# A state space layer of a two-block model at batch 256 tokens: the scans over pairs of tokens

## The chip, the cores and the metric

The kernel runs on one core of a Trainium2 chip. Its time is the device time of one execution in microseconds; of several executions the median is given. A core has the engines TensorE (PE in the profile, its weight loads are PEld), VectorE (DVE), ScalarE (ACT), GpSimd (POOL) and SyncE (SP), which issues most of the transfers. Each works off a queue of its own in order, and they wait for each other by semaphores.

## The reference

The model has two FFN layers around an even and an odd mixer, and two further layers behind. The change is in the odd mixer's state space half (S5). It has 32 groups of 16 channels and 64 complex states; the kernel lays two of them on the 128 partitions and calls these 32 channels and 128 states one of its 16 groups. S is 256 tokens.

```python
u = zd.reshape(B, S, S5_GROUPS, S5_GROUP_CH).astype(jnp.float32)
lam = lax.complex(lam_re, lam_im)
dt = jnp.exp(log_dt)[:, None]
lam_bar = jnp.exp(lam * dt)
b_bar = ((lam_bar - 1.0) / lam)[..., None] * b_c
bu = jnp.einsum('gpc,bsgc->sbgp', b_bar, u.astype(jnp.complex64))
a = jnp.broadcast_to(lam_bar, (S, 1, S5_GROUPS, S5_STATE))
def combine(e1, e2):
    a1, b1 = e1
    a2, b2 = e2
    return a2 * a1, a2 * b1 + b2
_, states = lax.associative_scan(combine, (a, bu), axis=0)
y = jnp.einsum('gcp,sbgp->bsgc', c_c, states).real + d_skip * u
y = jax.nn.gelu(y.reshape(B, S, S5_WIDTH))
ab = y @ w_glu
y_d = ab[..., :S5_WIDTH] * jax.nn.sigmoid(ab[..., S5_WIDTH:])
return jnp.concatenate([y_c, y_d], axis=-1) @ w_out
```

So the state after token t is `lam_bar` times the state after t-1, plus `b_bar` times the token's input, and a token's output is the real part of C times its state, plus `d_skip` times its input. The other half of the mixer, `y_c`, is a pooling branch.

## The kernel before

All work is on one core and all 256 tokens are columns of one tile. Big products are split into a high and a low fp32r part of activation and weight (`xh`, `xl`, `wh`, `wl`, three matmuls a product; L251 is the helper that issues every such matmul). ScalarE makes `wh` (L160) and VectorE `wl` (L161) out of `raw`, which SyncE fetches (L143).

`s5_params` prepares the constants of the S5 half. It is a generator: `run` hands it to two FFN layers (`ffn1(0, 1)` and `ffn1(1, 0)`, until 690 us), which take a step of it at each `yield`, so that its work lies between theirs. For each of 16 groups i it makes a table `tab` with the sine and cosine of the state's angle at each of the 256 tokens (L729 to L737), further `rho` (the modulus of `lam_bar`), `fr`, `fi` (the factor of `b_bar`), `bexp` and out of it by transposes `bt` (the matrix of the drive, L775, L777), and `cw` (the matrix of the read, three copies: real, minus imaginary, minus real; fetched at L779, changed at L780 and L781).

`odd` is the mixer, from 690 to 809 us. Its input projections come first; `u` (tile `s5u`) is the S5 half's input, times the norm's factor `R` (L796). Then a loop of 19 steps runs over the 16 groups as a software pipeline. A group's steps are:

- `drive`: f32 matmuls out of 32 partitions of `u` (for two groups at a time, on two row groups of TensorE, into two PSUM banks).
- `turn`: VectorE multiplies the two halves of that PSUM bank with the table (L820, L821, 128x512), which turns the complex state back by its angle.
- `scan`: a sum and a difference (L825, L826), then two scans over 256 columns with the real factor `rho` (L829, L830). GpSimd multiplies one of the results with the table (`zi`, L832).
- `back`: VectorE does so with the other (`zr`, L838).
- `read`: four f32 matmuls with `cw` into 32 rows of `py`, a column group of TensorE (L844).
- `finish`, after each fourth group: `d_skip` (L849), gelu (L850), and the split into `yh`, `yl` (L267, L269).

Turnings of group n, the turning back of n-1, scans of n and the read of n-2 are issued in this order in step n. After each step one step of `pooling` is issued, the pooling branch: first its projection of the input (512 columns), then for each of four groups a product with the pooling matrix, `pl` (ScalarE, L869), a product with `pw`, `yc` (ScalarE, L873) and its halves `ch`, `cl` (L267, L269), and last `od_w_out` over `ch`, `cl`. After the loop come the gate's matmuls (`s5_w_glu` over `yh`, `yl`) and the second half of `od_w_out`. The scheduler of the framework sets the order on each engine out of what the code issues, so steps of one tile are moved among those of another.

## Time and profile before

| what | us |
| --- | --- |
| median of 3 runs (lowest, highest) | 3098.61 (3095.78, 3099.87) |
| profiled execution | 3096.39 |
| its span on the chip | 3094.6 |
| TensorE busy in the span | 3000.1 (97%) |
| VectorE busy | 2317.8 (75%) |
| ScalarE busy | 1874.5 (61%) |
| from `s5u` (L796) to the first matmul of the second `od_w_out` half | 706.26 to 797.78 |

Times in the profile count from the start of the span. An instruction's row gives its start, its length, engine, line, what it writes and reads (`out<-in`), the shape, and how many it stands for (x4: four in a row). In brackets stands for how long the engine had been idle before it, and who released it. Matmuls are pipelined, so the distance from start to start counts, not the length; an f32 matmul leaves two records, an fp32r one leaves one.

### The profile page before, as it was taken

Reading aid. Unit: us, or ns where it says so; the run is one execution under the profiler, and the core shown is the slowest. Engines: PE = TensorE matmul, PEld = TensorE weight load, DVE = VectorE, ACT = ScalarE, POOL = GpSimd, SP = SyncE. Lnnn points to the kernel's source line nnn. Section 1 sums busy time; section 2 is a strip of 40 time slices with the busy share of each in tenths; the row PEclk is TensorE's granted clock in tenths of the full one; section 3 lists DMA queues with packets and bytes.
Section 4 is the critical chain, followed back from the end, with each engine's and each line's share of the span. In section 5 each row is a group of like instructions: output and inputs, shape, how many; then the busy total and the mean of one; then the engine's idle time right before and its main releaser. Section 6 shows DMA issues by size and latency. Waiting matters only on the chain. (4 is left out here: it accounts for less than half of the span.)

```text
span 3094.6 us, 51454 instructions
## 1 busy us (share of the span) xinstructions
PE 3000.1 (97%) x20681; PEld 2715.5 (88%) x20681; DVE 2317.8 (75%) x3292; ACT 1874.5 (61%) x2593; POOL 174.9 (6%) x147
## 2 busy tenths in 40 slices
PE   8999999999999999999999999999999999999998
PEld 8997999995899889899998888988888887888886
DVE  6667787868775675566556665569999999999998
ACT  5556555552444665554546654458788778778776
POOL 1000000002102000012010000000000000000000
PEclk9999999999999999999999999999999999999999
DMA  6542455551455334454553334658998998999994
GB/s 254 205 163 99 180 187 181 200 212 57 164 191 194 123 126 147 167 192 163 191 191 123 124 134 180 235 218 316 363 371 335 364 358 343 363 363 342 358 370 157
DMA packets 97413, 696.49 MB, mean 225 GB/s; under 512 B 10880, under 2 KB 11232, under 8 KB 13456
## 3 DMA queue, kind: packets, MB, share of 16 engines
q1 hardware_dynamic: 95184, 685.81, 59.9%
q0 software_dynamic: 752, 3.98, 0.4%
q8 instruction: 164, 2.69, 0.3%
q10 hardware_dynamic: 1232, 3.34, 0.3%
q14 instruction: 81, 0.66, 0.1%
HBM read 692.05 MB, written 1.05 MB: 224 GB/s over the span
## 5 line engine op out<-in xcount | busy, mean ns | idle before, releaser
L161 DVE TENSOR_TENSOR wl<-raw,wh 128x1024 fp32r<-128x1024 f32 x1299 | 1580.4, 1236 | 491.4 <-ACT wh L160 456.5
L160 ACT ACTIVATE wh<-raw 128x1024 fp32r<-128x1024 f32 x1299 | 1361.9, 1060 | 762.0 <-PE pa L251 633.8
L251 PE MATMUL pa<-xh,wh 128*128 128x256 f32 x3072 | 862.4, 281 | 13.2 <-ACT wh L160 9.8
L251 PE MATMUL pa<-xl,wh 128*128 128x256 f32 x3072 | 860.6, 280 | 4.0 <-DVE xl L349 4.0
L251 PE MATMUL pa<-xh,wl 128*128 128x256 f32 x3072 | 858.7, 280 | 0.9 <-DVE wl L161 0.9
L251 PEld LDWEIGHTS pa<-xh,wh 128*128 128x128 f32 x3072 | 581.4, 189 | 18.1 <-ACT wh L160 9.8
L251 PEld LDWEIGHTS pa<-xl,wh 128*128 128x128 f32 x3072 | 581.5, 189 | 6.7 <-DVE xl L349 5.0
L251 PEld LDWEIGHTS pa<-xh,wl 128*128 128x128 f32 x3072 | 585.1, 190 | 1.9 <-DVE wl L161 1.5
L251 PE MATMUL pa<-wl,gxh 128*128 128x512 f32 x896 | 349.7, 390 | 1.6 <-DVE wl L161 1.5
L251 PE MATMUL pa<-wh,gxl 128*128 128x512 f32 x896 | 348.8, 389 | 0.0
L251 PE MATMUL pa<-wh,gxh 128*128 128x512 f32 x896 | 317.1, 389 | 0.0
L251 PE MATMUL pa<-hh,wl 128*128 128x256 f32 x880 | 245.2, 279 | 0.0
L251 PE MATMUL pa<-hl,wh 128*128 128x256 f32 x880 | 245.2, 279 | 0.0
L251 PE MATMUL pa<-hh,wh 128*128 128x256 f32 x880 | 245.0, 278 | 0.0
L251 PEld LDWEIGHTS pa<-wl,gxh 128*128 128x128 f32 x896 | 168.2, 188 | 40.1 <-DVE wl L161 5.2
L251 PEld LDWEIGHTS pa<-wh,gxh 128*128 128x128 f32 x896 | 168.1, 188 | 35.1
L251 PEld LDWEIGHTS pa<-wh,gxl 128*128 128x128 f32 x896 | 168.2, 188 | 34.6
L251 PE MATMUL pb<-wl,mhh 128*128 128x512 f32 x448 | 177.2, 396 | 1.1 <-DVE wl L161 1.1
L251 PE MATMUL pb<-wh,mhl 128*128 128x512 f32 x448 | 176.0, 393 | 0.0
L251 PEld LDWEIGHTS pa<-hh,wl 128*128 128x128 f32 x880 | 165.9, 189 | 0.1
L251 PEld LDWEIGHTS pa<-hl,wh 128*128 128x128 f32 x880 | 165.7, 188 | 0.0
L251 PEld LDWEIGHTS pa<-hh,wh 128*128 128x128 f32 x880 | 165.7, 188 | 0.0
(512 smaller groups left out, 3987.6 us busy)
## 6 DMA issues: line engine op xcount, KB each, us to landing
raw<-in_moe SPq DMA_DIRECT2D x336, 1024.0 KB, 6.2
raw<-in_dense SPq DMA_DIRECT2D x315, 1024.0 KB, 4.8
c_lay<-in_c_lay POOLq DMA_DIRECT2D x2, 1216.0 KB, 6.6
x<-in_xt SPq DMA_DIRECT2D x4, 256.0 KB, 5.6
raw<-in_dense SPq DMA_DIRECT2D x4, 256.0 KB, 6.7
w<-in_cw ACTq DMA_DIRECT2D x1, 1024.0 KB, 8.1
out_dram<-hx SPq DMA_DIRECT2D x2, 512.0 KB, 2.6
c_odd<-in_c_odd POOLq DMA_DIRECT2D x1, 768.0 KB, 4.5
```

What stands on the lines that cost most here:

```text
L160: self.nc.scalar.activation(h, src, AF.Copy)
L161: self.nc.vector.tensor_sub(l, src, h)
L251: self.nc.tensor.matmul(out, l, r, start=start, stop=stop, skip_group_check=True)
```

## The change

The state is now carried over two tokens at a time: 128 columns, one for each pair of tokens. With s(t) the state after token t, s(2m+1) = lam_bar^2 s(2m-1) + lam_bar b u(2m) + b u(2m+1). So

- `u` is stored by parity: [128, 4, 2, 128], first tokens and second tokens of all pairs (four VectorE products of 256 instead of two of 512).
- A second drive matrix with the factor `lam_bar` b (`gr`, `gi`) is made: `bexp1`, and `bt` holds both. A drive of two groups is eight matmuls of 128 columns (tokens 1 and 0 accumulated) instead of four of 256.
- `tab`, and all steps that make it, are 128 columns wide. The values of `lam_bar` come from a short calculation of their own (`one`) instead of 32 products of one column out of `tab`; `rho` is squared.
- `turn`, `scan`, `back` and `zi` take two groups at once: four turnings of 256 elements, a sum and a difference over both groups (2x128), four scans of 128 columns, one `zi` and one `zr` of 512. The loop has 10 steps, and takes two steps of `pooling` in each.
- `back` now joins `zr` and `zi` into one tile by a difference and a sum (L887, L888), so that a read is two matmuls a group and token. Second tokens are read by `cw`, first tokens by `cl` (C times `lam_bar`) from the state of the pair ahead of them (127 columns), and a direct product `d0` (C times b, a 128x128 matrix for each four groups) times the first tokens' input. `cl` costs six VectorE operations of 128x512, `d0` 32 matmuls of 32x32 at the boundary of FFN and mixer, and four copies by ScalarE; `cw` has no third copy any more.
- `cw` is fetched right after `s5b` and not after the transposes.
- `finish` writes `y` with a stride of two.
- `free=384` instead of 128 moves addresses alone.

```diff
+        tab = P2.tile([128, 16, 2, 128], F32, name="tab")
...
+        nc.scalar.activation(one[:, 1], one[:, 0], AF.Sin, scale=2 * math.pi * (1 - 2.0 ** -22))
+        io = io[:, 0:S:2]
...
+        cw = P2.tile([128, 2, 16, 32], F32, name="cw")
+        tc.keep_in_program_order(nc.scalar.dma_start(cw, self.a["s5c"]))
...
+        bt = P2.tile([128, 2, 2, 4, 128], F32, name="bt")
+        for tok, (mr, mi) in enumerate(((fr, fi), (gr, gi))):
...
+            bexps.append(bexp)
+            yield
+            for ri in range(2):
+                pt = self.pbank((128, 4, 128))
+                for j in range(4):
+                    nc.tensor.transpose(pt[:, j], bexp[:, ri, 4 * j:4 * j + 4].rearrange("p a b c -> p (a b c)"),
+                                        self.ident)
+                nc.scalar.activation(bt[:, tok, ri], pt, AF.Copy)
...
-        cw = P2.tile([128, 3, 16, 32], F32, name="cw")
-        tc.keep_in_program_order(nc.scalar.dma_start(cw[:, 0:2], self.a["s5c"]))
+
+
         V.tensor_scalar_mul(cw[:, 1], cw[:, 1], -1.0)
-        V.tensor_scalar_mul(cw[:, 2], cw[:, 0], -1.0)
-        self.s5 = dict(rho=rho_t, tab=tab, bt=bt, cw=cw)
+        cl = P2.tile([128, 2, 16, 32], F32, name="cl")
+        ct = P.tile([128, 16, 32], F32, name="s5ct")
+        bc = lambda v: v[:, :, None].to_broadcast([128, 16, 32])
+        for ri, op in enumerate((OP.add, OP.subtract)):
+            V.tensor_mul(cl[:, ri], cw[:, ri], bc(lr1))
+            V.tensor_mul(ct, cw[:, 1 - ri], bc(li))
+            V.tensor_tensor(cl[:, ri], cl[:, ri], ct, op=op)
+        yield
+        d0 = P2.tile([128, 4, 128], F32, name="d0")
+        tc.keep_in_program_order(nc.gpsimd.memset(d0, 0.0))
+        pt = self.pbank((128, 4, 32))
+        for i in range(16):
+            j, q = divmod(i, 4)
+            for ri in range(2):
+                nc.tensor.matmul(pt[32 * q:32 * q + 32, j], bexps[0][:, ri, i].rearrange("p b c -> p (b c)"),
+                                 cw[:, ri, i], start=j == 0 and ri == 0, stop=j == 3 and ri == 1,
+                                 skip_group_check=True, tile_position=(0, 32 * q))
+        for q in range(4):
+            r = slice(32 * q, 32 * q + 32)
+            nc.scalar.activation(d0[r, :, r], pt[r], AF.Copy)
+        self.s5 = dict(rho=rho_t, tab=tab, bt=bt, cw=cw, cl=cl, d0=d0)
...
-            u = P.tile([128, 4, S], F32, name="s5u")
+
+            u = P.tile([128, 4, 2, 128], F32, name="s5u")
+            apart = lambda t: t.rearrange("p (t r) -> p r t", r=2)
             bs = [self.proj_t([(w, idx, 512 + 256 * i, 256)], self.xh, self.xl) for i in range(2)]
             rc, R = factors()
             for i in range(2):
-                nc.vector.tensor_mul(u[:, 2 * i:2 * i + 2], bs[i], R[:, None, :].to_broadcast([128, 2, S]))
+                for n in range(2):
+                    nc.vector.tensor_mul(u[:, 2 * i + n], apart(bs[i][:, n]), apart(R))
...
-                bus = [self.pbank((128, 2, S)) for _ in range(2)]
+                bus = [self.pbank((128, 2, 128)) for _ in range(2)]
                 for ri in range(2):
-                    for n, bu in enumerate(bus):
-                        j, q = divmod(i + n, 4)
-                        r = slice(32 * q, 32 * q + 32)
-                        self.mm(bu[:, ri], s5["bt"][r, ri, j], u[r, j], True, True)
+                    for tok in range(2):
+                        for n, bu in enumerate(bus):
+                            j, q = divmod(i + n, 4)
+                            r = slice(32 * q, 32 * q + 32)
+                            self.mm(bu[:, ri], s5["bt"][r, tok, ri, j], u[r, j, 1 - tok], ri == 0 and tok == 0, tok == 1)
...
-            def turn(i, bu):
-
-                tb = s5["tab"][:, i]
+                return P.tile([128, 2, 2, 128], F32, name=n, tag="s5w", bufs=9)
+
+            def both(v):
+                return v[:, :, None, :].to_broadcast([128, 2, 2, 128])
+
+            def turn(i, bus):
+
                 a1, a2 = work("a1"), work("a2")
-                V.tensor_mul(a1, bu[:, 0, None, :].to_broadcast([128, 2, S]), tb)
-                V.tensor_mul(a2, bu[:, 1, None, :].to_broadcast([128, 2, S]), tb)
+                for n, bu in enumerate(bus):
+                    for ri, a in enumerate((a1, a2)):
+                        V.tensor_mul(a[:, n], bu[:, ri, None, :].to_broadcast([128, 2, 128]), s5["tab"][:, i + n])
                 return a1, a2
 
             def scan(i, a1, a2):
-                V.tensor_add(a1[:, 1], a1[:, 1], a2[:, 0])
-                V.tensor_sub(a1[:, 0], a2[:, 1], a1[:, 0])
+                V.tensor_add(a1[:, :, 1], a1[:, :, 1], a2[:, :, 0])
+                V.tensor_sub(a1[:, :, 0], a2[:, :, 1], a1[:, :, 0])
                 z = a2
-                rho = s5["rho"][:, i:i + 1].to_broadcast([128, S])
-                V.tensor_tensor_scan(z[:, 1], rho, a1[:, 0], 0.0, OP.mult, OP.add)
-                V.tensor_tensor_scan(z[:, 0], rho, a1[:, 1], 0.0, OP.mult, OP.add)
+                for n in range(2):
+                    rho = s5["rho"][:, i + n:i + n + 1].to_broadcast([128, 128])
+                    V.tensor_tensor_scan(z[:, n, 1], rho, a1[:, n, 0], 0.0, OP.mult, OP.add)
+                    V.tensor_tensor_scan(z[:, n, 0], rho, a1[:, n, 1], 0.0, OP.mult, OP.add)
                 zi = work("zi")
-                nc.gpsimd.tensor_mul(zi, z[:, 1, None, :].to_broadcast([128, 2, S]), s5["tab"][:, i])
+                nc.gpsimd.tensor_mul(zi, both(z[:, :, 1]), s5["tab"][:, i:i + 2])
                 return z, zi
 
             def back(i, z, zi):
 
                 zr = work("zr")
-                V.tensor_mul(zr, z[:, 0, None, :].to_broadcast([128, 2, S]), s5["tab"][:, i])
-                return zr, zi
-
-            def read(i, zr, zi, py):
-                o = py[32 * (i % 4):32 * (i % 4) + 32, :S]
-                for n, (c, z) in enumerate(((0, zr[:, 1]), (1, zr[:, 0]), (2, zi[:, 0]), (1, zi[:, 1]))):
-                    nc.tensor.matmul(o, cw[:, c, i], z, start=n == 0, stop=n == 3, skip_group_check=True,
-                                     tile_position=(0, 32 * (i % 4)))
+                V.tensor_mul(zr, both(z[:, :, 0]), s5["tab"][:, i:i + 2])
+                V.tensor_sub(zr[:, :, 1], zr[:, :, 1], zi[:, :, 0])
+                V.tensor_add(zr[:, :, 0], zr[:, :, 0], zi[:, :, 1])
+                return zr
+
+            def read(i, zr, py):
+
+                if i % 4 == 0:
+                    self.mm(py[:, 0], s5["d0"][:, i // 4], u[:, i // 4, 0], True, False)
+                for ri in range(2):
+                    for c, o, t in ((cw, py[:, 1], 128), (s5["cl"], py[:, 0, 1:128], 127)):
+                        for n in range(2):
+                            q = 32 * ((i + n) % 4)
+                            nc.tensor.matmul(o[q:q + 32], c[:, ri, i + n], zr[:, n, 1 - ri, 0:t], start=False,
+                                             stop=ri == 1, skip_group_check=True, tile_position=(0, q))
 
             def finish(j, py):
                 y = W.tile([128, S], F32, name="y", tag="t256", bufs=4)
-                V.scalar_tensor_tensor(y, u[:, j], self.vec("s5d", j), py[:, :S], op0=OP.mult, op1=OP.add)
+                V.scalar_tensor_tensor(apart(y), u[:, j], self.vec("s5d", j), py, op0=OP.mult, op1=OP.add)
...
+            z, x, py = {}, {}, None
+            for m in range(8 + 2):
+                i = 2 * m
+                if m < 8:
+                    a = turn(i, drive(i))
+                if 0 <= m - 1 < 8:
+                    x[m - 1] = back(i - 2, *z.pop(m - 1))
+                if m < 8:
+                    z[m] = scan(i, *a)
+                if 0 <= m - 2 < 8:
+                    i -= 4
                     if i % 4 == 0:
+                        py = self.pbank((128, 2, 128))
+                    read(i, x.pop(m - 2), py)
+                    if i % 4 == 2:
+                        finish(i // 4, py)
+                for _ in range(2):
+                    next(steps, None)
```

What moves in the order, at three places (`pb` and `pa` are PSUM banks). TensorE at the boundary from the FFN (`pa<-hh`) to the mixer's first projection (`pa<-xh`), before:

```order
L251 MATMUL pa_8213<-hh_6082,wl_8303 128x256
L775 MATMUL pb_8378<-c_all_101,bexp_8199 128x128 [waits Pool_49]
L775 MATMUL pb_8378<-c_all_101,bexp_8199 128x128 x3
L775 MATMUL pb_8384<-c_all_101,bexp_8199 128x128 x4
L251 MATMUL pa_8421<-xh_108,wh_8302 128x256 [waits PE_49]
```

and after:

```order
L251 MATMUL pa_8198<-hh_6087,wl_8288 128x256
L795 MATMUL pb_8362<-c_all_101,bexp0_8186 128x128 [waits Pool_49]
L795 MATMUL pb_8362<-c_all_101,bexp0_8186 128x128 x3
L795 MATMUL pb_8368<-c_all_101,bexp0_8186 128x128 x4
L795 MATMUL pb_8387<-c_all_101,bexp1_8374 128x128 [waits DVE_49,Pool_49]
L795 MATMUL pb_8387<-c_all_101,bexp1_8374 128x128 x3
L795 MATMUL pb_8393<-c_all_101,bexp1_8374 128x128 [waits DVE_49]
L795 MATMUL pb_8393<-c_all_101,bexp1_8374 128x128 x3
L816 MATMUL pb_8410<-cw_8181,bexp0_8186 32x32 [waits DMAHW1_49,Activation_49]
L816 MATMUL pb_8410<-cw_8181,bexp0_8186 32x32 x31
L251 MATMUL pa_8473<-xh_108,wh_8287 128x256
```

The second matrix's transposes and the products of `d0` (L816) now stand ahead of the projection; they wait for VectorE's copies into `bexp1` and for `cw`.

VectorE in the loop, one group of before (`a1`, `a2` are the turned drives):

```order
L820 TENSOR_TENSOR a1_8621<-pb_8615,tab_4455 128x512
L821 TENSOR_TENSOR a2_8622<-pb_8615,tab_4455 128x512
L838 TENSOR_TENSOR zr_8625<-a2_8594,tab_4455 128x512 [waits DVE_49]
L825 TENSOR_TENSOR a1_8621<-a1_8621,a2_8622 128x256 [waits DVE_49]
L826 TENSOR_TENSOR a1_8621<-a2_8622,a1_8621 128x256
L830 SCALAR_TENSOR_TENSOR a2_8622<-rho_4417,a1_8621 128x256 [waits DVE_49]
L829 SCALAR_TENSOR_TENSOR a2_8622<-rho_4417,a1_8621 128x256 [waits DVE_49]
```

and the sixth pair of after (`cl` from `yc` is a half of the pooling branch, not the matrix of the read):

```order
L269 TENSOR_TENSOR cl_8622<-yc_8872,ch_8621 128x256 [waits Activation_49]
L269 TENSOR_TENSOR cl_8622<-yc_8883,ch_8621 128x256 [waits Activation_49]
L868 TENSOR_TENSOR a1_8919<-pb_8909,tab_4455 128x256 [waits PE_49]
L868 TENSOR_TENSOR a2_8920<-pb_8909,tab_4455 128x256
L269 TENSOR_TENSOR cl_8622<-yc_8894,ch_8621 128x256 [waits Activation_49]
L868 TENSOR_TENSOR a1_8919<-pb_8910,tab_4455 128x256 [waits PE_49]
L868 TENSOR_TENSOR a2_8920<-pb_8910,tab_4455 128x256
L886 TENSOR_TENSOR zr_8925<-a2_8835,tab_4455 128x512 [waits DVE_49]
L872 TENSOR_TENSOR a1_8919<-a1_8919,a2_8920 128x2x128 [waits DVE_49]
L269 TENSOR_TENSOR cl_8622<-yc_8905,ch_8621 128x256 [waits Activation_49]
L887 TENSOR_TENSOR zr_8925<-zr_8925,zi_8850 128x2x128 [waits DVE_49,Pool_49]
L888 TENSOR_TENSOR zr_8925<-zr_8925,zi_8850 128x2x128
```

Four halves of the pooling branch, which wait for ScalarE, now stand among the turnings of this one pair.

TensorE in the loop, a drive and a read of before:

```order
L251 MATMUL pb_8673<-s5u_8420,bt_8377 128x256
L844 MATMUL pb_8633<-zr_8625,cw_8390 32x256 [waits DVE_49]
L844 MATMUL pb_8633<-zr_8625,cw_8390 32x256
L844 MATMUL pb_8633<-zi_8603,cw_8390 32x256 [waits Pool_49]
L844 MATMUL pb_8633<-zi_8603,cw_8390 32x256
```

and after:

```order
L251 MATMUL pb_8765<-s5u_8472,bt_8185 128x128
L251 MATMUL pb_8766<-s5u_8472,bt_8185 128x128
L899 MATMUL pb_8739<-zr_8727,cw_8181 32x128 [waits DVE_49]
L899 MATMUL pb_8739<-zr_8727,cw_8181 32x128
L899 MATMUL pb_8739<-zr_8727,cl_8400 32x127 x2
L899 MATMUL pb_8739<-zr_8727,cw_8181 32x128 [waits DVE_49]
L899 MATMUL pb_8739<-zr_8727,cw_8181 32x128
L899 MATMUL pb_8739<-zr_8727,cl_8400 32x127 x2
```

The matmuls of two groups now alternate, and no read waits for GpSimd, since VectorE joins `zi` to `zr`.

## Rows read from the trace of the kernel before

**Rows 1.** windows; length, busy us (instructions) by engine, TensorE's clock, DMA share, GB/s

```profile
225.00:233.00 8.00, 8.00 (x44) 8.00 (x44) 3.71 (x9) 2.12 (x5) 0.00 (x0) 0.57 0.48 172
...
706.00:789.00 83.00, 75.76 (x377) 46.67 (x375) 72.48 (x133) 18.78 (x31) 26.30 (x16) 1.00 0.13 46
```

**Rows 2.** groups by line, 706 to 789, TensorE; busy, mean | idle ahead

```profile
L844 PE MATMUL pb<-zr,cw 128*32 128x256 f32 x64 | 16.8, 384 | 3.3 <-DVE zr L838 2.1 <-issue 1.2
...
L251 PE MATMUL pb<-s5u,bt 32*128 32x256 f32 x64 | 14.9, 402 | 1.1 <-DVE a L821 1.0
```

**Rows 3.** groups by line, same stretch, VectorE

```profile
L849 DVE SCALAR_TENSOR_TENSOR y<-s5u,vecs,pb 128x256 f32<-128x256 f32 x3 | 1.4, 480 | 8.6 <-PE pb L844 8.6
```

**Rows 4.** timeline, VectorE and TensorE, one group of the loop; start, length, instruction

```profile
741.82 0.68 DVE L820 TENSOR_TENSOR a<-pb,tab 128x512 f32<-128x512 f32 x1
...
743.02 0.68 DVE L838 TENSOR_TENSOR zr<-a,tab 128x512 f32<-128x512 f32 x1
...
743.62 0.41 DVE L825 TENSOR_TENSOR a<-a,a 128x256 f32<-128x256 f32 x1
...
744.20 1.05 PE L844 MATMUL pb<-zr,cw 128*32 128x256 f32 x4
744.29 0.68 DVE L830 TENSOR_TENSOR_SCAN a<-rho,a 128x256 f32<-128x256 f32 x1
...
744.89 0.66 DVE L829 TENSOR_TENSOR_SCAN a<-rho,a 128x256 f32<-128x256 f32 x1
745.09 1.03 PE L844 MATMUL pb<-zi,cw 128*32 128x256 f32 x4
```

**Rows 5.** timeline, TensorE, drives of a pair

```profile
708.62 0.52 PEld L251 LDWEIGHTS pb<-s5u,bt 32*128 32x128 f32 x6 [0.24 <-issue]
...
708.62 1.13 PE L251 MATMUL pb<-s5u,bt 32*128 32x256 f32 x8
...
709.68 0.50 PE L251 MATMUL pa<-wh,xh 128*128 128x512 f32 x1
...
715.69 1.12 PE L251 MATMUL pb<-s5u,bt 32*128 32x256 f32 x4
```

**Rows 6.** timelines, TensorE, narrow products of the even mixer

```profile
209.24 2.05 PE L251 MATMUL pb<-blk,w 128*64 128x30 f32 x32
...
253.56 0.66 PE L251 MATMUL pb<-p,vt 128*64 128x128 f32 x8
...
254.15 0.71 PE L251 MATMUL pb<-ksw,qt 64*128 64x128 f32 x8
```

**Rows 7.** timeline, TensorE, a product of the pooling branch; the second od_w_out half's start

```profile
752.35 0.70 PE L251 MATMUL pa<-pl,pw 128*128 128x256 f32 x2 [0.98 <-ACT pl L869]
...
797.78 0.28 PE L251 MATMUL pa<-ch,wh 128*128 128x256 f32 x1
```

**Rows 8.** one line's instructions, GpSimd; ns least/median/most, first and last start

```profile
L832 POOL TENSOR_TENSOR zi<-a,tab x16: 1267/1283/2682, 711.9 to 785.2; 128x512 f32<-128x512 f32 x16
```

**Rows 9.** timeline at the mixer's start, all engines

```profile
689.53 1.04 PE L775 MATMUL pb<-c_all,bexp 128*128 128x128 f32 x8
...
690.32 0.36 PE L251 MATMUL pa<-xh,wh 128*128 128x256 f32 x1
...
699.15 0.43 DVE L780 TENSOR_SCALAR cw<-cw 128x512 f32<-128x512 f32 x1 [6.51 <-DMA cw<-in_s5c]
...
699.82 4.63 DVE L161 TENSOR_TENSOR wl<-raw,wh 128x1024 fp32r<-128x1024 f32 x4
...
701.10 0.38 PE L251 MATMUL pa<-xh,wl 128*128 128x256 f32 x1 [0.41 <-DVE wl L161]
...
705.38 0.43 PE L321 MATMUL pb<-c_all,rsr 128*128 128x128 f32 x2 [1.25 <-POOL rsr L314]
```

**Rows 10.** windows, in the FFN ahead

```profile
660.00:680.00 20.00, 20.00 (x178) 20.00 (x178) 12.15 (x18) 8.81 (x12) 1.42 (x1) 1.00 0.47 179
```

**Rows 11.** one line's instructions, TensorE's weight loads of the reads

```profile
L844 PEld LDWEIGHTS pb<-zr,cw x64: 106/109/110, 713.8 to 787.5; 128*32 128x32 f32 x64
```

71 lines of the change are left out of this document (28 added, 43 removed).

## The prediction

> **What bounds the kernel now.** The order of reading was: the windows of the odd stage, then its groups by line, then the timeline of one iteration. Ahead of the stage TensorE is full and after it again; the reader should look at the 83 us from 706 to 789 alone, where TensorE is busy 75.76 us and VectorE 72.48 us at full clock, with the DMA engines at 0.13 [rows 1]. So two engines are almost full at once, in a loop in which each waits for the other in turn: TensorE waits for `zr` and for a PSUM bank that `a` is read from [rows 2], VectorE stands 8.6 us, three times, ahead of `y` for the last read of four groups [rows 3]. A cut of one engine alone would be stopped by the other; what counts is whether the change cuts both. The chain of waits carries nothing inside this window, so the sums below go by the two engines and by a walk through the new order.
>
> **VectorE in the loop.** One group of before costs, start to start [rows 4]: two turnings and the turning back of 128x512 at 0.60 us, two sums of 256 columns in 0.67, two scans of 256 at 0.60: 3.67 us. A pair costs 7.33. After, a pair is four turnings of 256 elements, two sums and two differences of 2x128, four scans of 128 columns, and one turning back of 512. An operation of 256 elements has the row of the sum, 0.67 / 2 = 0.334; no scan of 128 columns is in this trace, and 512 to 256 elements fell from 0.60 to 0.334, so a scan, with 0.60 at 256 columns, should fall alike to 0.334 (between 0.30, an exact half, and 0.60, if length didn't matter, which would be +8.5 us over 32 scans; I take 0.334, by the row that has the same two lengths). Pair: 12 x 0.334 + 0.60 = 4.61. Saved: 8 x 2.72 = **21.8 us** out of 58.7. GpSimd's product `zi` keeps its size and is issued eight times instead of sixteen.
>
> **TensorE in the loop.** An f32 matmul leaves two records. The read of a group is four matmuls, eight records of 256 columns: `zr` at 744.20, `zi` at 745.09, so 0.89 for each four, 1.78 a group [rows 4], 28.5 us for sixteen. After, a pair has 16 records of 127 or 128 columns, alternating between two column groups of 32. At half the columns a record is 0.108; where the two column groups run side by side, 16 records take 8 x 0.108 and some 0.25 for the switch into that shape (the weight load of a drive after other work has 0.24 of waiting ahead of it [rows 5]), together 1.1. Rows for that: eight records of `pb<-p,vt` in two column groups of 64 run from 253.56 to 254.15, 0.59 us, well under 8 x 0.108 [rows 6]. Where they take turns it is 16 x 0.108 + 0.1 = 1.8. I take 1.1, nearest to that row: 8.8 us, saved 19.7.
> The drives: a pair was eight records of 256 columns, on two row groups side by side, 1.06 us where it is issued whole (708.62 to 709.68), and two halves of about 1.1 each where another tile's work lies between [rows 5]; three whole and five split make 14.2. After, it has twice as many records of half the columns, so the same 1.1; the order has six whole and two split: 11.0, saved 3.2. The four direct products `d0` are new, two records of 128 columns and a switch each, 4 x 0.3 = 1.2 more. Sum: **-21.7 us** of 75.8.
>
> **The walk.** Both engines lose the same 22 us, so the loop should lose at least near that; whether waits eat it, I tried by laying each instruction of the new order down at these durations, with 0 where `s5u` starts (706.26). Turnings of the eight pairs start at 2.5, 5.8, 10.5, 16.3, 22.5, 28.5, 38.8 and 45.2. In the sixth VectorE stands: its queue has the halves `cl` of the pooling branch between scans and turnings, and these wait for ScalarE's `yc`, which waits for TensorE's `pl` product (before, that chain cost TensorE 0.98 us at 752.35 [rows 7]); I count 2.6 us and 0.4 there. The last read ends at 55.3 and the gate matmuls behind the loop at 64, where before `od_w_out` starts at 797.78 [rows 7], 91.5 after `s5u`: -27. It is more than 22 since three waits of VectorE for the last of four reads get shorter. A walk sees no late semaphores and no uneven GpSimd (the `zi` of before took 1.27 to 2.68 us [rows 8]), so I give 2 us back: **-25**.
>
> **Ahead of the loop.** The boundary from the FFN to the stage is TensorE's, and everything added there lies on the path:
> - eight more transposes: eight stand from 689.53 to the next matmul at 690.32 [rows 9]. +0.8.
> - 32 matmuls of 32x32 for `d0`, 64 records with a weight load each. The nearest row has 32 records of 30 columns in 2.05 us, 0.059 each after the first [rows 6]: 64 x 0.059 = 3.8, and 0.3 for two switches. Two of these records are one product, and four column groups follow on each other, so it may be as little as 1.9. I take 3.8.
> - The second matrix `bexp1`: VectorE builds it, and `cl`, between the weight halves `wl` of the last FFN steps, about 6 us of new work there. A walk along its order has `bexp1` ready near 691.5 and TensorE at its second transposes near 690.4: +1 (0 to 2).
> - Against it, `cw` is fetched right behind `s5b`. In before VectorE waited 6.51 us for it at 699.15, did then four `wl` in a row, and TensorE stood 0.41 for one of these at 701.10 and 1.25 for `rsr` at 705.38, since the `rsv` ahead of it was queued behind the four [rows 9]. With the fetch behind `s5b`, ahead of VectorE's work on `bexp`, both should go: -1.4 (I leave 0.3 of it).
> Sum **+4.5**, between +1.5 and +6.
> The Trainium skill (TensorE: Matmul & The Clock Gate, section "Wait — 56ns, not 53.3ns?") gives about 25 ns as the least distance of small matmuls; by it the 64 records would take 1.6 us, and the whole sum would be 2 us lower. The row of 30 columns, at 59 ns, speaks against that here.
>
> **Priced at nothing.** The tables of half the length, and the sixteen pairs of tiny products that become two, lie under an FFN in which TensorE is busy 20.00 of 20 us and VectorE 12 [rows 10]; cover remains. The order of SyncE's queue is the same, and behind the stage every engine's order is that of before. The DMA engines idle in the loop since the buffers of weights are full, so an earlier end lets them start earlier too.
>
> **Sum.** -25 + 4.5 = -20.5. Against the profiled execution of 3096.39 us that is 3076; on the median of the runs, 3098.61, **3078**. The kernel's runs spread 4 us; about 0.2%, 6 us, is what can be told from no change.
>
> **Rivals.**
> *Waits take the work's place.* VectorE's queue runs in order; if it waits behind `cl`, `y` or PSUM banks in each pair and not in one, an iteration costs the round trip drive, turning, scan, `zi`, back, read, and not 4.61. Speaking for it: before, TensorE already stood 3.3 us ahead of the reads and 1.1 ahead of the drives [rows 2]. Against it: the walk finds VectorE with work in its queue in seven pairs of eight. Two more us in each of six iterations: -20.5 + 12, some **3090**.
> *Narrow columns don't run side by side.* Reads at 1.8 a pair, 8 x 0.7 = +5.6 if all of it is on the path: **3084**. The Trainium skill (TensorEngine Tiling (Array Packing), section Restrictions) says that column tiling switches fast weight loading off, and loads that take turns would do the same to narrow matmuls. The loads of the reads of before took 0.109 us [rows 11], just what a record of 128 columns takes, and the row of `p,vt` stands against their taking turns.
> *Slower: the clock.* TensorE's clock was 1.00 through the stage, but 0.57 in the window 225 to 233 though it was busy throughout, and 44 matmuls stand in these 8 us where an FFN window at full clock has 178 in 20 [rows 1, 10]. With shorter matmuls and waits between them the loop could fall to the lower level, 1.2 GHz. Each us of TensorE work then costs one more; the loop has 54 of it, so from 20 us at the low level on the change loses. All of the loop: -20.5 + 54, **3132**; two thirds of it, 3114.
> *Nothing comes through.* The gain is taken back by a later stage that runs at the pace of the DMA queues: 3096. Against it stands that these queues wait for buffers in the loop.
>
> **How the numbers follow.** The forecast, 3078, has 0.70 (3071 to 3083 by its terms: scans, `d0`, friction). Waits 0.14, narrow columns 0.07, clock 0.05, nothing 0.04. The range of 8 in 10 is 3069 to 3090: it leaves out the worse half of the waits (0.07), the clock, nothing, and a little of the forecast's own spread below. Faster by over 0.2% (under 3092.4): the forecast, narrow columns and nearly all of the waits, 0.90; within 0.2%: nothing, and a rest of the waits, 0.05; slower: the clock, 0.05.
>
> **What would show it.** In the changed kernel's trace: a pair's VectorE operations at 4.6 us and scans near 0.334 start to start; 16 read records in 1.1 us, with pairs of starts a few ns apart; TensorE's time from `s5u` to the first `od_w_out` matmul of the second half near 66 us; 64 small records in 3.8 us; no wait for `cw`; granted clock 1.00 in the stage. It would be wrong if scans cost as much as before, if the clock fell, or if VectorE shows waits of more than 1 us in most pairs.

## The result, and the profile of the changed kernel

| what | before | changed |
| --- | --- | --- |
| median of 10 runs each (lowest, highest), us | 3099.24 (3093.96, 3113.07) | 3062.02 (3057.23, 3087.05) |
| profiled execution, us | 3096.39 | 3057.23 |
| its span, us | 3094.6 | 3055.5 |

The ratio is 0.989, interval 0.9873 to 0.9907. The forecast was 3078 with a range of 3069 to 3090: the direction was right, and the time lies 7 us below the range. Between the two profiled executions 39.1 us of span are gone, where the sum had 20.5.

To see where, the start of each weight half `wh` (ScalarE's product of L160) was compared: there are 1299 of them in the same sequence in both kernels, so the n-th is the same place of the program. At 688 us, before the stage, the changed kernel is already 7.5 us ahead; over the stage (the 228th to the 254th `wh`, 139.6 us before, 114.1 after) it gains 25.5; and the rest comes far behind it, mostly between 1740 and 2050 us of the run before. So the 39.1 have two parts, one in the stage, one outside it.

**The stage is what was predicted.** Below is the stage of the changed kernel, from `s5u` to the end of the gate's matmuls, as one window (length, busy us and instructions by engine, TensorE's clock, DMA share, GB/s):

```profile
700.60:764.60 64.00, 60.35 (x523) 51.20 (x522) 62.09 (x137) 23.61 (x40) 10.39 (x8) 1.00 0.24 86
```

VectorE is now busy 62.09 of 64 us and TensorE 60.35. In [rows 1] VectorE had 10.5 us of slack in 83; now it has 2 in 64, and the clock is still 1.00. Taken from `s5u` (start) to the start of the last gate matmul, the stage fell from 91.41 to 63.82 us: -27.6.

One pair's instructions on VectorE, from the timeline (start, length, instruction; a second group of rows is the read that lies beside it on TensorE):

```profile
706.49 1.39 DVE L868 TENSOR_TENSOR a<-pb,tab 128x256 f32<-128x256 f32 x4
...
707.80 0.68 DVE L886 TENSOR_TENSOR zr<-a,tab 128x512 f32<-128x512 f32 x1
...
708.39 0.42 DVE L872 TENSOR_TENSOR a<-a,a 128x256 f32<-128x256 f32 x1
708.73 0.42 DVE L887 TENSOR_TENSOR zr<-zr,zi 128x256 f32<-128x256 f32 x1
709.07 0.42 DVE L888 TENSOR_TENSOR zr<-zr,zi 128x256 f32<-128x256 f32 x1
...
709.40 0.42 DVE L873 TENSOR_TENSOR a<-a,a 128x256 f32<-128x256 f32 x1
...
709.74 0.42 DVE L878 TENSOR_TENSOR_SCAN a<-rho,a 128x128 f32<-128x128 f32 x1
...
710.07 0.71 DVE L877 TENSOR_TENSOR_SCAN a<-rho,a 128x128 f32<-128x128 f32 x2
...
710.70 0.40 DVE L878 TENSOR_TENSOR_SCAN a<-rho,a 128x128 f32<-128x128 f32 x1
...
711.02 1.39 DVE L868 TENSOR_TENSOR a<-pb,tab 128x256 f32<-128x256 f32 x4
```

```profile
714.26 0.41 PE L899 MATMUL pb<-zr,cw 128*32 128x128 f32 x4
714.50 0.39 PE L899 MATMUL pb<-zr,cl 128*32 128x127 f32 x4
714.72 0.39 PE L899 MATMUL pb<-zr,cw 128*32 128x128 f32 x4
714.93 0.39 PE L899 MATMUL pb<-zr,cl 128*32 128x127 f32 x4
715.25 0.51 PE L251 MATMUL pa<-wh,xh 128*128 128x512 f32 x1
```

From one pair's turnings to the next are 711.02 - 706.49 = 4.53 us (predicted 4.61; a group in [rows 4] took 3.67, a pair 7.33). A scan of 128 columns takes 0.33 us from start to start. The 16 records of a read take 715.25 - 714.26 = 0.99 us, where [rows 4] has 0.89 for half of one group's read.

**The boundary from the FFN to the stage** is the place where the sum was too dear. TensorE there, from the timeline (in brackets the idle time ahead and who ended it):

```profile
682.00 1.47 PE L795 MATMUL pb<-c_all,bexp 128*128 128x128 f32 x12
...
684.81 0.66 PE L795 MATMUL pb<-c_all,bexp 128*128 128x128 f32 x4 [1.34 <-DVE bexp L789]
...
685.40 0.86 PE L816 MATMUL pb<-cw,bexp 128*32 128x32 f32 x64
686.18 0.39 PE L251 MATMUL pa<-xh,wh 128*128 128x256 f32 x1
...
699.73 0.43 PE L321 MATMUL pb<-c_all,rsr 128*128 128x128 f32 x2 [0.29 <-POOL rsr L314]
```

The wait for `bexp1` is there, 1.34 us. The 64 small records of `d0` take 0.79 us to the start of the next product (685.40 to 686.18) and not 4.1, and the wait for `rsr` fell from 1.25 [rows 9] to 0.29. From the 228th `wh` to `s5u` it was 18.0 us before and is 19.9 now: +1.9, where the sum had +4.5. This place differs from execution to execution: from the last matmul of the FFN to `s5u`, three executions of the kernel before (those of the table below) take 16.9, 16.2 and 15.3 us and four with the changed loop 18.7, 19.2, 19.1 and 17.0, in which the wait for `bexp1` is 1.34, 1.63, 1.55 and 0. On the mean the boundary costs +2.4.

**Outside the stage it is the pace of matmuls.** A matmul of 256 columns follows the one ahead of it after either 0.113 or 0.118 us, and keeps to the one or the other, with few exceptions, until TensorE's stream of them is broken by a wait or by another kind of product. Windows of 20 us in the two FFN layers ahead of the stage (columns as above; the number behind the first x... is the count of matmuls, and TensorE is full in all of them) show it. Before:

```profile
440.00:460.00 20.00, 20.00 (x172) 20.00 (x171) 13.47 (x23) 9.48 (x13) 0.00 (x0) 1.00 0.55 190
560.00:580.00 20.00, 20.00 (x179) 20.00 (x178) 16.15 (x29) 11.06 (x18) 0.00 (x0) 1.00 0.54 192
```

The changed kernel:

```profile
440.00:460.00 20.00, 20.00 (x179) 20.00 (x178) 14.64 (x25) 10.36 (x16) 0.00 (x0) 1.00 0.54 197
560.00:580.00 20.00, 20.00 (x179) 20.00 (x179) 15.46 (x27) 10.96 (x19) 0.00 (x0) 1.00 0.55 207
```

With the clock at 1.00 and nothing waited for, the same FFN did 172 matmuls in 20 us in the one execution and 179 in the other. Between 332 and 511 us 1515 matmuls stood 4.5 ns farther apart in the execution of before: 6.8 us. Counted over the whole span, matmuls at the longer pace cost the profiled execution of before 22.1 us (their number times 4.5 ns) and that of the changed kernel 7.2. So of the 39.1 us, 14.9 are pace, 25.5 are the stage, and the two together are 1.3 too many, which I could not place.

### The profile page after: what moved, and what is told of

It reads as the page before. It is cut to its first block, busy times and chain, and to the rows that moved or that the text cites. A ratio compares the mean times of both kernels' runs of the same rounds, so it can differ in the third digit from the quotient of the medians.

```text
span 3055.5 us, 51722 instructions
## 1 busy us (share of the span) xinstructions
PE 2964.7 (97%) x20825; PEld 2699.4 (88%) x20825; DVE 2295.6 (75%) x3280; ACT 1873.1 (61%) x2601; POOL 160.6 (5%) x141
## 5 line engine op out<-in xcount | busy, mean ns | idle before, releaser
L160 ACT ACTIVATE wh<-raw 128x1024 fp32r<-128x1024 f32 x1299 | 1361.7, 1061 | 726.3 <-PE pa L251 599.2
```

What stands on the lines that cost most here:

```text
L160: self.nc.scalar.activation(h, src, AF.Copy)
```

## The experiments

The first question was whether the change brought the better pace (its tables, its waits or the moved address of `free=384`), or whether an execution falls into one or the other. The kernel before, unchanged, with the unchanged changed kernel beside it, tells that apart.

**e1_before_again**: the kernel before, no edit.

> The kernel before, unchanged. In its trace the 256-column fp32r matmuls of the FFN from 299 to 511 us follow each other at 117.8 ns, those of the next FFN (522 to 690) at 113.3 ns; in the changed kernel's trace both have 113.3. Theory A (the pace belongs to the program: its addresses or its instruction sequence): the same stretches at 117.8 again, the start-to-start mean from 332 to 500 us stays 117.8. Theory B (the pace is drawn anew at each wait of TensorE, by chance of timing): other stretches are slow this time; 332 to 500 us may show 113.3, and the time then falls by some 7 us.

3102.47 us (10 runs) against 3102.99 (25 runs of the same kernel), ratio 0.9989 (0.9969 to 1.001). Its profiled execution had 18.7 us of the longer pace and not 22.1, partly elsewhere. Its windows:

```profile
440.00:460.00 20.00, 20.00 (x173) 20.00 (x172) 13.54 (x23) 9.73 (x14) 0.00 (x0) 1.00 0.63 210
560.00:580.00 20.00, 20.00 (x179) 20.00 (x178) 16.11 (x31) 11.33 (x18) 0.00 (x0) 1.00 0.60 211
```

In these two windows the paces are those of the first execution, as theory A has it. Other stretches changed, though the program is the same: 373 matmuls from 949 us on now had the shorter pace and 950 from 1297 us the longer one, both the other way round than before.

**e2_after_again**: the changed kernel, no edit.

> The changed kernel, unchanged. Theory A: 113.3 ns from 333 to 501 us again, ratio near 0.989 in each round. Theory B: single executions move by some 7 us with the pace of that FFN (1500 matmuls by 4.5 ns), and part of the 37 us between the medians is chance, the part of the odd stage (-25.6 in the traces) is not.

3075.34 us (10 runs, 3073.82 to 3095.78), ratio 0.9921 (0.99 to 0.9941): the same kernel, 13 us slower than in its first runs. The stage was 63.84 us, as in the first execution (63.82); the longer pace cost 27.1 us and not 7.2. Its windows look like those of the kernel before:

```profile
440.00:460.00 20.00, 20.00 (x172) 20.00 (x171) 14.11 (x24) 10.34 (x16) 0.00 (x0) 1.00 0.50 166
560.00:580.00 20.00, 20.00 (x179) 20.00 (x178) 15.32 (x26) 11.48 (x18) 0.00 (x0) 1.00 0.55 189
```

So the pace of the FFN at 440 us is not a property that the change brings.

**e3_before_free384** and **e4_after_free128**: the address alone, put into the kernel before, and taken back out of the changed one.

```diff
-                self.ffn1(0, 1, steps, free=128)
-                self.ffn1(1, 0, steps, free=128)
+                self.ffn1(0, 1, steps, free=384)
+                self.ffn1(1, 0, steps, free=384)
```

> The kernel before with the one number of the change that only moves addresses: free=384 instead of 128, which shifts hh and hl of two FFNs by 256 bytes. Theory A with addresses as the cause: the pace from 332 to 500 us changes to 113.3 or the next FFN's changes to 117.8; time moves by 7 us or more. Theory B, or A with the instruction sequence: nothing that the other runs of before don't show too.

> The changed kernel with free=128 as before, so that hh and hl lie 256 bytes lower. If this address is what keeps the FFNs at 113.3 ns, 333 to 501 us falls back to 117.8 and the time rises by 7 us or more (to 3069 or above). If not, 3062 as the changed kernel.

e3: 3103.41 us, ratio 1.0002 (0.9982 to 1.0022). e4: 3075.2 (4 runs), ratio 0.9911 (0.9876 to 0.9945), with a stage of 63.84 us. The address moves neither median, and both paces occur with either address. In e3 both FFNs ran at the longer pace, which cost 35.5 us in the whole span:

```profile
440.00:460.00 20.00, 20.00 (x172) 20.00 (x171) 15.73 (x29) 10.78 (x17) 0.00 (x0) 1.00 0.49 165
560.00:580.00 20.00, 20.00 (x172) 20.00 (x171) 15.77 (x30) 11.41 (x19) 0.00 (x0) 1.00 0.51 182
```

**e9_after_third**: the changed kernel once more, in another set of runs with its own runs of the kernel before.

> The changed kernel once more, on another occasion. Two occasions gave medians of 3062 and 3075 (before: 3099 and 3103), the stage being 63.8 us in each trace. Theory B (a stretch's pace, 113.3 or 117.8 ns, is drawn by chance at a wait): the median lies anywhere between 3060 and 3080, the trace's stage is 63.8 again, and the span less the excess of slow stretches (4.5 ns a matmul) is 3046 to 3050 as in the three traces so far. Theory A (3062 is the kernel's time, and the 3075 was a bad occasion): 3062.

3058.5 us (4 runs: 3058.2 to 3069.6), ratio 0.9864 (0.9834 to 0.9894). The three medians of one and the same kernel are 3062.0, 3075.3 and 3058.5, and the ratio's intervals of the second and the third do not meet. The 3058.5 lies 1.5 us below the range that theory B gave; the span without the longer pace lies within the 3046 to 3050 that it named (3046.7). In its profiled execution the first FFN has the short pace and the second the long one, a fourth pattern after those above:

```profile
440.00:460.00 20.00, 20.00 (x179) 20.00 (x178) 14.30 (x25) 10.71 (x17) 0.00 (x0) 1.00 0.58 202
560.00:580.00 20.00, 20.00 (x172) 20.00 (x171) 15.35 (x29) 11.10 (x20) 0.00 (x0) 1.00 0.57 197
```

The spans, what the longer pace cost in them, the difference of the two, and the stage:

| execution | span | longer pace | difference | stage |
| --- | --- | --- | --- | --- |
| before | 3094.6 | 22.1 | 3072.5 | 91.41 |
| e1 (before) | 3093.8 | 18.7 | 3075.1 | 91.33 |
| e3 (before, address) | 3114.8 | 35.5 | 3079.4 | 91.60 |
| changed | 3055.5 | 7.2 | 3048.2 | 63.82 |
| e2 (changed) | 3073.3 | 27.1 | 3046.2 | 63.84 |
| e4 (changed, address) | 3070.7 | 22.7 | 3047.9 | 63.84 |
| e9 (changed) | 3067.7 | 21.0 | 3046.7 | 63.83 |

Spans differ by 21 us within one kind and by 18 in the other; without the pace by 7 and by 2. The mean of the differences is 3075.7 before and 3047.3 changed: **-28**, of which the stretch with the stage has -25.2 (138.9 to 113.7 on the mean of the same executions). The other 3 us lie far behind it, between 1330 and 2120 us. There, with the pace taken out, the three executions of before take 786.8, 790.4 and 791.0 us and the four of the changed kernel 785.4 to 787.0: executions of one kernel differ there by more than these 3 us, and it is not shown that the change brings them. So the change's own worth is 25 us, or 28 if they are its own. All runs together say -32 (53 runs of before, mean 3101.9; 24 of the changed kernel, 3069.5, with a deviation of 10 us for one run), which lies near to it, with the pace in it.

The runs of one set agree more than they would if each execution drew its pace for itself: of the changed kernel's first ten runs nine lie under 3068, e2's ten all lie above 3073, and three of e9's four lie within half a microsecond of each other, while 25 runs of the kernel before in one set spread from 3088.8 to 3119.6. e1 to e4 ran on one chip, e5 to e8 on another and e9 to e12 on a third; the 1515 matmuls of the first FFN had the longer pace in all traces of e1 to e4 and the shorter one in all of e5 to e8. Only the first execution of a set left a trace. So the chip, or something else that a set shares, may have a part in the pace; no run tells.

**e10_more_breaks**: if a break of the stream draws the pace anew, more breaks should give a mix of both paces inside one FFN. A product of two columns, out of a copy of TensorE's last result, stands behind every third projection of the two FFNs, 14 in all; nobody reads it.

```diff
+                if free == 384 and f % 3 == 1:
+                    tiny = self.wk.tile([128, S], F32, name="tiny", tag="t256", bufs=4)[:, 0:2]
+                    self.tc.keep_in_program_order(nc.vector.tensor_copy(tiny, b[:, 0, 0:2]))
+                    self.tc.keep_in_program_order(nc.tensor.matmul(self.pbank((128, 2)), self.ones, tiny, start=True, stop=True,
+                                                                   skip_group_check=True))
```

> The changed kernel with one tiny f32 matmul of 2 columns after every third projection of the two FFNs from 290 to 690 us, fourteen in all, each waiting for a VectorE copy of the projection just done, so that the streams of 1500 matmuls are broken into pieces of some 140. Theory B: fast and slow pieces lie mixed in 300 to 500 and in 520 to 690 us, about one third slow. Rival (the pace belongs to the stretch or to the execution): each FFN has one pace, as in all traces so far.

3095.7 us (1 run); the stage is 63.82. (The breaks themselves cost some 19 us: the span less the longer pace is 3066.1, and 3047 without them.) Of 14 pieces behind such a product 4 have the longer pace. Two windows of 14 us, two pieces of the first FFN:

```profile
362.00:376.00 14.00, 14.00 (x121) 14.00 (x120) 8.79 (x12) 7.06 (x10) 0.00 (x0) 1.00 0.55 186
380.00:394.00 14.00, 14.00 (x126) 14.00 (x125) 11.69 (x40) 6.97 (x10) 0.00 (x0) 1.00 0.48 163
```

121 and 126 matmuls in 14 us, in one layer: the pace changes at a break and holds until another. Over eight traces (the seven of the table and e10), counting stretches of at least 15 matmuls, one of the short pace was followed by a short one 225 times and by a long one 101 times; a long one by a short one 102 times and by a long one 64 times. So about a third is long, whatever came before (31 and 39%). It is not a third everywhere: over all 14 traces of this case, the 440 matmuls that start at 1840 us in the kernel before had the longer pace 13 times, and the 142 that start at 1725 us never, while the 1515 and the 1477 of the two FFNs had it in 6 of the 13 traces in which they are not broken up. So the place in the program has a part in it. What decides it at a break stays open: in a long stretch the weight load and its matmul stand some 115 ns apart and in a short one 110, but that is the difference itself and not its cause.

The next four runs take the sum's terms apart.

**e5_read_serial**: are the narrow columns of the read side by side? The same 16 records, one group's eight first and then the other's.

```diff
-                for ri in range(2):
-                    for c, o, t in ((cw, py[:, 1], 128), (s5["cl"], py[:, 0, 1:128], 127)):
-                        for n in range(2):
-                            q = 32 * ((i + n) % 4)
+                for n in range(2):
+                    q = 32 * ((i + n) % 4)
+                    for ri in range(2):
+                        for c, o, t in ((cw, py[:, 1], 128), (s5["cl"], py[:, 0, 1:128], 127)):
```

> The changed kernel, but a pair's read issues all eight records of one group's column group and then those of the other, not the two in turn. Theory 'column groups run side by side when they alternate': a read goes from 1.0 us (714.26 to 715.25 in the changed kernel's trace) to 16 x 0.108 = 1.7 or more; the stage, from the start of s5u to the last matmul of the gate, 63.8 us in three traces of the changed kernel, grows by up to 8 x 0.75 = 6 if TensorE sets its pace, by under 2 if VectorE does. Rival 'they took turns anyway': read and stage as before.

A read by group, from the timeline of TensorE:

```profile
714.62 0.41 PE L899 MATMUL pb<-zr,cw 128*32 128x128 f32 x2
714.86 0.38 PE L899 MATMUL pb<-zr,cl 128*32 128x127 f32 x2
715.08 0.41 PE L899 MATMUL pb<-zr,cw 128*32 128x128 f32 x4
715.29 0.41 PE L899 MATMUL pb<-zr,cl 128*32 128x127 f32 x4
715.54 0.38 PE L899 MATMUL pb<-zr,cw 128*32 128x128 f32 x2
715.76 0.38 PE L899 MATMUL pb<-zr,cl 128*32 128x127 f32 x2
716.07 0.50 PE L251 MATMUL pa<-wh,xh 128*128 128x512 f32 x1
```

In the changed kernel the records of a pair's two groups start two by two, 6 to 7 ns apart. Here, from the first start to the next product, it is 1.45 us against 0.99. The 1.7 of the theory are not reached, since the middle rows still hold records of both groups: where one group's last half and the other's first meet, they run beside each other. The stage is 64.28 us, +0.46; 3070.96 us (1 run). Eight reads that are 0.46 longer would be 3.7 us in a row, so most of it lies under VectorE's work. The order of the columns is worth half a microsecond here, so the rival that has them take turns was priced far too high at +5.6, all of it on the path.

**e6_d0_serial**: what does one small record cost? The 64 records of `d0` column group by column group, so that a group's 16 records follow each other.

```diff
-        for i in range(16):
-            j, q = divmod(i, 4)
+        for n in range(16):
+            q, j = divmod(n, 4)
+            i = 4 * j + q
```

> The changed kernel, but the 32 small products of d0 at the boundary are issued column group by column group (eight products of one, then of the next) and not in turn. In the changed kernel their 64 records took 0.86 us, where 3.8 were forecast from the row of 30 columns (0.059 each). Theory 'they are cheap because four column groups run side by side': 64 records take 2 to 4 us here, and the time from the last FFN step to s5u grows by as much (20 us to 22 or 23). Rival 'a record of 32 columns is cheap in itself': 0.7 to 0.9 us again.

The line's records in e6 (durations least, median, most in ns, then first and last start in us):

```profile
L817 PE MATMUL pb<-cw,bexp x64: 196/196/217, 692.3 to 694.1; 128*32 128x32 f32 x64
```

and in the changed kernel:

```profile
L816 PE MATMUL pb<-cw,bexp x64: 196/196/217, 685.4 to 686.1; 128*32 128x32 f32 x64
```

From the first record to the next product it is 1.84 us in e6 against 0.79: in one column group a record of 32 columns costs 29 ns on the mean (31 is the median distance of two starts), and over four column groups in turn 12. The 1.84 us lie between the rival's 0.9 and the theory's 2. The sum took 59 from a row of 30 columns in another place and shape [rows 6]. The Trainium skill (TensorE: Matmul & The Clock Gate, section "Wait — 56ns, not 53.3ns?") gives some 25 ns as the least distance of small matmuls; the 29 ns of e6 are near to it, and the 12 ns of the changed kernel are below it, so here it holds for one column group and not for four in turn. The stage is 63.82 us and the run 3066.16 (1 run), with 15.6 us of the longer pace.

**e7_vector_back**: is VectorE's saving what pays? Per pair five dead VectorE products (4 x 0.60 + 0.33 us by their shapes, 2.7 in all, what a pair had saved) are added; nobody reads them.

```diff
+            dead = P.tile([128, 2, 2, 128], F32, name="dead")
+
             def scan(i, a1, a2):
+                for _ in range(4):
+                    V.tensor_mul(dead, a1, a2)
+                V.tensor_mul(dead[:, 0], a1[:, 0], a2[:, 0])
```

> The changed kernel with 2.7 us of dead VectorE products in each pair (four of 512 elements and one of 256, into a tile that nobody reads), so that VectorE's work in the loop is again that of before, and TensorE's is the smaller one. Theory 'both engines had to be cut': the stage (63.8 us; 91.4 before) goes back to 78 to 88. Rival 'TensorE alone was the bound': 64 to 68.

The stage is 90.85 us: +27.0 for 22 us of work, nearly all that the change had brought, and above the 78 to 88 that were expected; 3101.98 us (1 run). More than the work came back, so not all of it is VectorE's work. The windows of the stage:

```profile
707.00:728.00 21.00, 17.50 (x120) 12.61 (x118) 19.67 (x41) 7.02 (x9) 1.30 (x1) 1.00 0.31 110
728.00:734.00 6.00, 4.89 (x33) 4.14 (x33) 4.09 (x10) 0.06 (x1) 1.30 (x1) 0.55 0.34 142
734.00:760.00 26.00, 25.33 (x192) 21.56 (x191) 24.49 (x61) 10.19 (x19) 3.85 (x3) 0.97 0.01 1
760.00:780.00 20.00, 16.10 (x106) 14.38 (x105) 19.77 (x44) 1.90 (x3) 2.58 (x2) 0.74 0.15 54
780.00:798.00 18.00, 11.16 (x76) 10.01 (x76) 12.38 (x22) 2.80 (x5) 1.26 (x1) 0.72 0.16 58
```

TensorE waits more (11.16 busy of 18 in the last row), and its granted clock falls to 0.55 in the second row and to 0.72 to 0.74 in the last two, that is, to the lower level for part of them. A read then takes up to 1.7 us (its four quarters stand 0.43 apart and not 0.22), and VectorE waits for it: only 4.09 of 6 and 12.38 of 18 busy. The trace gives the account. VectorE's idle time in the stage rises from 1.9 to 10.4 us: 4.0 of it ahead of `y` for the reads, 5.3 for ScalarE. The time for which VectorE's operations are held by GpSimd's `zi` (the last section shows how) falls from 4.5 to 1.1. 22 + 8.5 - 3.4 is 27.1. How much of the 8.5 the clock brings, the run does not part.

**e8_tensor_back**: the same question for TensorE. Six dead f32 products of 256 columns per pair, into columns of the read's bank that nobody reads.

```diff
+                for _ in range(6):
+                    nc.tensor.matmul(py[:, 2:4], s5["d0"][:, i // 4], u[:, i // 4], start=False, stop=False,
+                                     skip_group_check=True)
...
```

> The changed kernel with six dead f32 matmuls of 256 columns in each pair, ahead of its read and into a part of the bank that nobody reads (12 records of 0.217 and two switches: 2.9 us), so that TensorE's work in the loop is about that of before and VectorE's is the smaller one. Theory 'both engines had to be cut': the stage goes from 63.8 to 78 to 88 us. Rival 'VectorE alone was the bound': 64 to 70.

The stage is 77.99 us, +14.2 for some 23 us of work; 3080.37 us (1 run). The stage as one window:

```profile
705.60:783.80 78.20, 78.20 (x618) 66.36 (x618) 62.78 (x141) 24.80 (x41) 10.32 (x8) 1.00 0.23 82
```

TensorE is full, at full clock, and VectorE (62.78 busy, as in the changed kernel) waits for it. So each engine alone, put back to near its old work, takes back half or more of the gain: both had to be cut.

The last two runs look for something better than both kernels, since VectorE is at 62.09 of 64.

**e11_read_apart**: no joining of `zr` and `zi` on VectorE (16 operations of 0.33 us less), twice the read's records on TensorE, with negated copies as before.

```diff
...
-                V.tensor_sub(zr[:, :, 1], zr[:, :, 1], zi[:, :, 0])
-                V.tensor_add(zr[:, :, 0], zr[:, :, 0], zi[:, :, 1])
-                return zr
+                return zr, zi
...
-                for ri in range(2):
+                for k, (ri, z, h) in enumerate(((0, zr, 1), (1, zr, 0), (2, zi, 0), (1, zi, 1))):
...
```

> The changed kernel, but VectorE no longer joins zi to zr (two operations of 2x128 less in each pair, 0.67 us): the read takes zr and zi apart, with third copies of cw and cl, 32 records a pair in place of 16 (0.9 us more TensorE). By the two runs that put work back, a us of VectorE's work moves the stage by 27.0 / 21.8 = 1.24 us and one of TensorE's by 0.2 to 0.6: 63.8 - 6.6 + 1.5 to 4.4 = 59 to 62 us. Rival (the read waits for GpSimd's zi again, as before the change): 64 to 67.

The stage is 65.29 us, +1.5; 3074.09 (4 runs), ratio 0.9903 (0.9865 to 0.9941). As one window:

```profile
706.30:771.80 65.50, 65.01 (x650) 56.80 (x650) 58.81 (x125) 25.21 (x41) 11.42 (x8) 1.00 0.27 97
```

VectorE lost 3.3 us of busy time, and TensorE, at 65.01 of 65.5, became the bound. The stage lies in the range of the rival that has the read wait for `zi`, but not for its reason: TensorE stands still for 0.5 us in all.

**e12_pool_add**: one of the two joinings on GpSimd.

```diff
-                V.tensor_add(zr[:, :, 0], zr[:, :, 0], zi[:, :, 1])
+                nc.gpsimd.tensor_add(zr[:, :, 0], zr[:, :, 0], zi[:, :, 1])
```

> The changed kernel with one of the two joining operations of each pair on GpSimd instead of VectorE. VectorE has 8 x 0.334 = 2.7 us less: 63.8 - 3.3 = 60.5 if only that counts. Rival: GpSimd's work slows VectorE's wl (1.2 us alone, up to 2.3 us beside zi in the changed kernel's trace) and the second half of the read waits for GpSimd: 64 to 67.

The stage is 67.44 us, +3.6; 3075.51 (1 run). The two joinings of e12:

```profile
L888 POOL TENSOR_TENSOR zr<-zr,zi x8: 727/760/2027, 721.8 to 768.7; 128x256 f32<-128x256 f32 x8
L887 DVE TENSOR_TENSOR zr<-zr,zi x8: 410/788/968, 721.9 to 769.1; 128x256 f32<-128x256 f32 x8
```

GpSimd takes 0.73 to 2.03 us for what VectorE did in 0.33, and VectorE's own joining beside it goes from 412 ns (median in the changed kernel) to 788. VectorE's busy time rose by 2.4 us though it has eight operations less: its operations are held by GpSimd's for 8.3 us in the stage and not for 4.5, and these 3.8 us are about what the stage lost. The end lies 0.4 us above the upper end of the rival's range.

e11 and e12 were expected to gain because I had read e7 as 1.24 us of stage for each us of VectorE; that number holds e7's waits, and both engines are too near to full for a cut that loads the other. By its stage, the changed kernel stayed the best of all that ran.

## Why the prediction came out as it did

- **The loop: its work right, its end in part by luck.** VectorE's pair 4.53 (4.61), scans 0.33 (0.334), the read 0.99 (1.1), 16 records of a drive 1.09 (1.1; from 701.25 to 702.34 in the timeline), clock 1.00. The walk's end of the gate, 64 after `s5u`, was met to 0.2 us (63.82 to 63.84 in six executions that have this loop). But its middle was not met. The turnings of the fourth, fifth and sixth pair start 17.2, 23.9 and 30.5 us after `s5u`, where the walk had 16.3, 22.5 and 28.5; the seventh pair's start at 38.9, with the walk again (38.8). Two errors offset each other. In pairs three to six, one VectorE operation each was held by the `zi` beside it, for 3.8 us together, of which the walk had nothing; and the 3.0 us that VectorE was to stand in the sixth pair are 0.23:

```profile
733.99 0.43 DVE L269 TENSOR_TENSOR cl<-yc,ch 128x256 fp32r<-128x256 f32 x1 [0.23 <-ACT ch L267]
```

  The 2 us that were given back for uneven GpSimd and late semaphores were right in kind, then, and too few (4.5 us are held in the whole stage); what made them an error is that the walk already had nearly 3 us of standing too much.
- **The boundary, too dear by 2 to 3 us.** `d0` at 4.1 us was the mis-sized term: 0.8 measured. I had written that it may be as little as 1.9, since column groups follow on each other, and then took the row of 30 columns, which has no column groups of 32 and no order in turn. The wait for `bexp1` (0 to 1.6 us in four executions, for +1) and the absent wait for `cw` were as said.
- **Priced at nothing, right as work.** With the pace taken out, from the start of the first FFN's long stretch under the generator's steps to that of the next FFN's, it is 215.0 to 215.4 us in three executions of before and 215.0 to 215.6 in four of the changed kernel. Tables of half the length gain nothing there.
- **The step that failed: the sum puts nothing for the pace, and takes its spread from three runs.** "The kernel's runs spread 4 us": these were three runs. The 53 runs of the kernel before lie between 3088.8 and 3119.6, one profiled execution has 7 to 36 us of the longer pace, and 15 us of the difference of the two profiled executions are that. The traces had shown it: [rows 10] is a window with 178 matmuls in 20 us, and other windows of the two FFN layers, as full, at the same clock, had 172. I read the one row as the state of the FFN and did not ask why a full engine at full clock does 172 in one window and 178 in another. The medians fell by 37.2 us and the sum had 20.5. Of the 16.7 between them the stage has 4.7: 2.6 in the loop, mostly the 2 that were given back, and 2.1 at the boundary. Some 3 lie where executions of one kernel differ as much. The remaining 9 are left for the pace by subtraction alone: the one traced execution of the ten had little of the longer pace (7.2 us), the nine others left no trace. The forecast's middle corrected by what was measured in the stage (-25.5) is 3073 and lies in the range, so the terms by themselves would not have missed it. A range of +-6 us for the terms needed another 10 or so for the pace.
- **The rivals.** Waits in each pair: none, VectorE is 97% busy. Columns in turn: e5 shows that they are side by side; it goes most of the way to turns (1.45 us a read, where the rival had 1.8) and costs 0.5 us of stage, not near 5.6. The clock: not in the changed kernel, but e7 shows that the mechanism exists; with 22 us more of VectorE's work in the loop TensorE waits more, and windows that hold half of the stage have a granted clock of 0.55 to 0.74. Nothing comes through: the lead of 33.1 us that the changed kernel has behind the stage is still there at the end of the profiled execution (39.1).

## What to carry to other kernels

When two engines are nearly full and wait for each other in turn, count both, and lay out the new order by hand: the walk's end was within 0.2 us where the sums of engines were 6 off. Compare such a walk with the trace at several places and not at its end alone; here two errors of about 3 us cancelled. Before giving a range, compare the same full stretch in several windows and executions: two counts of matmuls in equal full windows at the same clock are a spread of the whole kernel that no term of the change explains. And compare a change by the stage it touches, over several executions of both kernels, before a difference of the totals is believed.

## What the chip showed that I had not expected

- Matmuls of 256 columns follow each other after 0.113 or 0.118 us at the same granted clock, changing at breaks of the stream, about one time in three the longer, in some places nearly always and in some never; 7 to 36 us of a span of 3.1 ms.
- Small records in four column groups in turn cost 12 ns each, in one column group 29 (e6).
- VectorE's operations can be held by GpSimd's. In the changed kernel, two places from the timelines of the two engines:

```profile
715.46 1.30 POOL L880 TENSOR_TENSOR zi<-a,tab 128x512 f32<-128x512 f32 x1 [3.26 <-DVE a L877]
722.22 1.27 POOL L880 TENSOR_TENSOR zi<-a,tab 128x512 f32<-128x512 f32 x1 [5.46 <-DVE a L877]
```

```profile
715.55 2.29 DVE L161 TENSOR_TENSOR wl<-raw,wh 128x1024 fp32r<-128x1024 f32 x1
722.69 1.88 DVE L161 TENSOR_TENSOR wl<-raw,wh 128x1024 fp32r<-128x1024 f32 x1
```

  The first `zi` ends at 716.76 and the `wl` beside it 1.08 us after that; the second ends at 723.48 and its `wl` again 1.08 us after. A `wl` alone takes 1.22. All five `wl` of the stage that start beside a `zi` end 1.08 us after it, and a `cl` (0.41 alone) took 1.46 and ended 0.28 after its `zi`. So they are held until the `zi` is done; 4.5 us of VectorE's time in the stage are that, in e2 as well. The turnings, `y` and `x`, which read PSUM, show no such length beside a `zi`. It also goes the other way: in the kernel before, two `cl` at 754.49 kept their 0.42 us each, and the `zi` that had started 0.09 us before them took 2.01 and not 1.27. The Trainium skill (Trainium Architecture — The Big Picture, section "🎯 What this means for kernel authors") says that these two engines share a port, and that one locks the other out; the rows agree with it, and so do the joinings of e12.
